# The first rows of an encoder layer: who prepares them, who issues their loads, and in which order and banks they are multiplied

## The chip, the cores and the metric

The kernel runs on one core of a Trainium2 chip, as one launch. The metric is the device time of that launch in microseconds. Five engines work side by side and meet at semaphores: TensorE (PE in the profile, with its weight loads as PEld), VectorE (DVE), ScalarE (ACT), GpSimd (POOL) and SyncE (SP), which issues most DMA transfers. ACT and POOL can issue transfers too.

## The reference

One layer of a hybrid encoder over 512 tokens of width 1024, float32 in and out: a half-step SwiGLU feed-forward, a mixer (dilated window attention in three groups, grouped-query attention with axial rotary, both gated and merged), a second half-step SwiGLU, and a final normalisation.

```python
def rmsnorm(x, g):
    y = x * lax.rsqrt(jnp.mean(x * x, axis=-1, keepdims=True) + EPS)
    return y * g

def swiglu(x, w1, w3, w2):
    return (jax.nn.silu(x @ w1) * (x @ w3)) @ w2

x = x + 0.5 * swiglu(rmsnorm(x, ffn1_norm), ffn1_w1, ffn1_w3, ffn1_w2)
h = rmsnorm(x, mix_norm)
x = x + hybrid_mixer(h, ...)
x = x + 0.5 * swiglu(rmsnorm(x, ffn2_norm), ffn2_w1, ffn2_w3, ffn2_w2)
return rmsnorm(x, final_norm)
```

D_FF is 2816. Only the beginning of the first feed-forward is touched by the change.

## The kernel before

Activations are held transposed, as eight tiles x0 to x7 of 128 features by 512 tokens. Every matrix product is made of three products of a shorter float format (float32r): an operand is split into a high part H (a rounded copy) and a low part L (the rest), and a product is H·H + L·H + H·L. On PE the weights' part is the stationary operand and the activations' part, 512 columns, the moving one. In the rows below hH and hL are the parts of the activations scaled by the norm's gain, wh and wl those of the weights, and wr is the raw weight tile as it was loaded. ACT usually makes the high part, DVE the low part. The factor 1/rms of the norm is applied after the product (tile R).

`layer` (L1264 on) opens the kernel. It allocates two raw and two split weight tiles, issues a few warm-up products on a zeroed tile (`idle`, L269) and then goes through the eight feature tiles d. For each it issues the load of x, for d below 4 also the load of that row's weights (in two pieces of 256 columns for d = 0, in one of 512 for the others), scales x into hH on ACT and hL on DVE (`norm_h`, L410 and L411), and splits the weights (L1274 on ACT, L1275 on DVE). "Row d" below is the d-th eighth of the sum over the 1024 features, with 12 products.

The first four blocks of 128 output features are computed together by `quad`: four PSUM banks, and for each row d and each of the four blocks three products (`mm3`, L262 to L264). After 28 of the 32 steps of `quad` the statistics product (`stat_r`, L441) stands on PE; it reads the sum of squares that ACT and DVE make after the last hH. Two PSUM pools of four banks exist: `psm` for blocks (tile name mm) and `psa` (tag aux) for the warm-up, the statistics and others. `quad` takes all of `psm`. The fifth block (`feat` with aux set, in `plain`) takes a bank of `psa`, the sixth takes the next of `psm`, that is the first bank of `quad`, which is empty when DVE has multiplied it by R (`done1`, L509). R is ready only after the statistics, so the results of `quad` are held until then.

PE runs in the order of the program text. The instructions of the other engines are put in order by a scheduler when the program is built. SP issues one DMA after the other; eight semaphores are used in turn by all transfers of SP and ACT, and an issue waits until the transfer that used its semaphore before has landed.

The kernel goes on with the rest of the first feed-forward (with a Strassen-like scheme of seven products for eight), the mixer and the second feed-forward; none of these lines is changed.

Of the kernel before, what the change touches and what calls it, by code (L numbers as in the profile page):

```python
# [13 lines left out]
AF = mybir.ActivationFunctionType  # L14
ALU = mybir.AluOpType
# [16 lines left out]
GAP_B = 1  # L32
LAG = 1
LAST = 2
WARM = 4
T = 512
D = 1024
NK = 8
# [11 lines left out]
G_FFN1, G_MIX, G_FFN2, G_FIN, G_BG = 0, 8, 16, 24, 32  # L50
# [16 lines left out]
def f32(t):  # L67
    return t.bitcast(F32)


class Layer:
    def __init__(self, ctx, tc, a):
# [9 lines left out]
        nc = self.nc  # L82
        c = self.cst
# [7 lines left out]
        self.mhalf, self.eps = small[:, 0:4], small[:, 4:5]  # L91
        nc.vector.memset(self.mhalf, -0.5)
        nc.vector.memset(self.eps, EPS)
        nc.scalar.activation(self.ones, self.ones, AF.Copy)
        self.r = c.tile([128, 8], F32, name="r")
        self.R = c.tile([128, T], F32, name="R")
        nc.gpsimd.memset(self.R, 0.0)
# [189 lines left out]
    def quad(self, name, done):  # L287
        banks = [self.bank() for _ in range(4)]
        for k in range(NK):
            if k % 2 == 0:  # L290
                H, L = self.weights(name, k // 2)
            for c in range(4):
                s = slice(512 * (k % 2) + 128 * c, 512 * (k % 2) + 128 * c + 128)
                self.mm3(banks[c], H[:, s], L[:, s], self.hH[k], self.hL[k], k == 0, k == NK - 1)
                if k == NK - 1:
                    done[c](banks[c])
                yield

    def token(self, name, n, toks, done):
        banks = [self.bank() for _ in toks]  # L300
# [102 lines left out]
            for _ in range(n):  # L403
                next(fill, None)

    def norm_h(self, d, g, n=T):
        nc = self.nc
        gc = self.par[:, g + d:g + d + 1]
        H, L, x = self.hH[d][:, :n], self.hL[d][:, :n], self.x[d][:, :n]
        self.lead = nc.scalar.activation(H, x, AF.Copy, scale=gc)  # L410
        nc.vector.scalar_tensor_tensor(L, x, gc, f32(H), op0=ALU.mult, op1=ALU.subtract)  # L411

    def norm_sq(self, d, pool=NK - 2):
        nc = self.nc
# [67 lines left out]
    def ffn_run(self, s, gin, gnext, hooks, out=None, side={}):  # L482
        nc = self.nc
        g, t, c, half = [], {}, {}, []
# [79 lines left out]
        def later(fn):  # L564
            return lambda ps: fn(ps) if held is None else held.append((fn, ps))
# [3 lines left out]
        def plain():  # L569
            if s == "a":  # L570
                yield from self.quad("w13a", [later(fn) for fn in (done1, done3) * 2])
            for f in range(2, first):
                yield from self.feat("w13" + s, 2 * f, later(done1), f == 2)
                yield from self.feat("w13" + s, 2 * f + 1, later(done3))

        def add(x, ps, R):
            if R is None:
# [28 lines left out]
        lo, n = first, 0  # L606
        for gi, hi in enumerate(ends):
            last = hi == NF
# [16 lines left out]
            n, lo = n + NK * len(g), hi  # L625
# [25 lines left out]
        sqs, first = [], iter(())  # L651
        for hf in range(2):
# [19 lines left out]
            first = norm(hf)  # L672
# [584 lines left out]
    def layer(self, out):  # L1257
        nc, tc = self.nc, self.tc
        for n in range(2):
            self.raws[n] = self.ring("wr", self.todo.pop(0), 0, n)  # L1260
            self.tiles.append(self.ring("wh", n, 0, n))
        self.idle(WARM, 256)
        for d in range(NK):
            if d > 3 and d % 2 == 0:  # L1264
                self.load(self.todo.pop(0))
            nc.sync.dma_start(self.x[d], self.a["x"][d])
            w = 0 if d > 3 else 512 if d else 256
            parts = [slice(512 * (d % 2) + s, 512 * (d % 2) + s + w) for s in range(0, 512, w)] if w else []
            for s in parts:
                nc.sync.dma_start(self.raws[d // 2][:, s], self.a["w13a"][d // 2][:, s])  # L1270
            self.norm_h(d, G_FFN1)
            for s in parts:
                raw, (H, L) = self.raws[d // 2], self.tiles[d // 2]
                nc.scalar.copy(H[:, s], raw[:, s])  # L1274
                nc.vector.tensor_sub(L[:, s], raw[:, s], f32(H)[:, s])  # L1275
        nc.sync.dma_start(self.ident, self.a["ident"])

        def squares():
            with tc.issue_after(self.lead.ins):
                for d in range(NK):  # L1280
                    self.norm_sq(d, 0)

        with tc.tile_pool(name="bt", bufs=1, side="right") as bp:
            hooks = {16: squares, 27: self.stat_r, 33: self.stat_R, "T": (22, 2)}
            self.bias_open(bp)
            side = {(0, d): lambda g=d: self.bias_rows(g) for d in range(3)}
            for h in range(8):
                side[(0, 4 + h) if h < 4 else (1, h - 4)] = lambda h=h: self.bias_spread(h)
            with ExitStack() as ctx:
                self.ffn_open(ctx, "a")  # L1290
                self.ffn_run("a", G_FFN1, G_MIX, hooks, side=side)
                self.freed = None
                self.wx = None
        self.fctx = ExitStack()
        self.mixer()
        self.ffn_run("b", G_FFN2, G_FIN, {3: self.stat_r, 5: self.stat_R}, out)
        self.wx = None
        self.fctx.close()
        self.hctx.close()
# [100 lines left out]
```

## Time and profile before

| | us |
|---|---|
| median of 3 runs (lowest, highest) | 1244.58 (1244.53, 1245.4) |
| profiled execution, its own time | 1244.16 |
| its span in the profile | 1242.4 |
| PE busy | 1233.9 (99%) |
| DVE busy | 906.8 (73%) |
| ACT busy | 605.8 (49%) |
| DMA, mean over the span | 154 GB/s |

The span goes from the first to the last instruction in the trace; the execution's own time holds 1.76 us more. In the rows of the timeline stand the start in us, the duration, the engine, the line, the operation, and what it writes and reads; "xN" is a count of merged instructions, and brackets at the end tell how long the engine had been idle and what ended that. ACTq, SPq and POOLq rows are issues of DMA transfers.

### The profile page before, as it was taken

How to read it: one execution, taken by the hardware profiler on the slowest of the kernel's cores; microseconds unless marked ns; L12 is line 12 of the kernel's file. 1: busy time of each engine (PE TensorE's matmuls, PEld its weight loads, DVE VectorE, ACT ScalarE, POOL GpSimd, SP SyncE). 2: the span in 40 equal slices, each digit the busy share in tenths (PEclk: the TensorE clock that was granted, in tenths of full speed). 3: DMA queues.
4: the chain of work that ended last, by engine and by line, in shares of the span. 5: the costliest groups of instructions: out<-in, count | busy, mean ns of one | idle time of the engine just before them, and what ended most of it. 6: DMA issues, size and time to landing. Idle time of an engine off the chain costs nothing.

```text
span 1242.4 us, 20511 instructions
## 1 busy us (share of the span) xinstructions
PE 1233.9 (99%) x8228; PEld 1116.0 (90%) x8228; DVE 906.8 (73%) x1371; ACT 605.8 (49%) x897; POOL 126.5 (10%) x131
## 2 busy tenths in 40 slices
PE   9999999999999999999999999999999999999998
PEld 7897999899899999988888888888899989988997
DVE  6985688468787887567746888865988757875874
ACT  7652365245464444454424446664665425532554
POOL 1111101000222110200001200000211001100001
PEclk9999999999999999999999999999999999999999
DMA  8785777241388982662232231267768536744222
GB/s 292 220 217 166 194 195 194 92 119 52 136 222 251 231 229 97 223 183 79 87 116 100 68 119 43 71 218 241 208 170 203 157 99 188 189 149 111 60 85 68
DMA packets 90224, 190.85 MB, mean 154 GB/s; under 512 B 12801, under 2 KB 18577, under 8 KB 90129
## 3 DMA queue, kind: packets, MB, share of 16 engines
q1 hardware_dynamic: 70912, 145.46, 34.5%
q0 software_dynamic: 18496, 43.54, 17.6%
q8 instruction: 64, 1.05, 0.4%
q10 hardware_dynamic: 720, 0.55, 0.1%
q14 instruction: 32, 0.25, 0.1%
HBM read 175.79 MB, written 17.38 MB: 155 GB/s over the span
## 4 chain that ended last, share of the span: by engine, by line
PE 92%; DVE 3%; DMA 2%; issue 1%; ACT 0%; SPq 0%; POOL 0%; POOLq 0%; ACTq 0%; DVEq 0%
PE mm L262 23%; PE mm L264 22%; PE mm L263 22%; PE Y L263 4%; PE Y L262 4%; PE Y L264 4%; PE X L263 2%; PE X L264 2%; PE X L262 2%; DMA wt<-in_w13b 1%; PE S L925 1%; PE mm L1001 1%; PE Tb L1137 1%; PE T L1012 1%; DVE wl L248 1%
## 5 line engine op out<-in xcount | busy, mean ns | idle before, releaser
L247 ACT CAST wh<-wr 128x1024 fp32r<-128x1024 f32 x133 | 139.6, 1050 | 182.2 <-PE mm L263 124.1
L248 DVE TENSOR_TENSOR wl<-wr,wh 128x1024 fp32r<-128x1024 f32 x133 | 163.0, 1225 | 52.1 <-ACT wh L247 51.5
L262 PE MATMUL mm<-hH,wh 128*128 128x256 f32 (+1 forms) x560 | 179.7, 321 | 0.4 <-DVE t L509 0.3
L264 PE MATMUL mm<-hH,wl 128*128 128x256 f32 (+1 forms) x560 | 177.0, 316 | 0.0
L263 PE MATMUL mm<-hL,wh 128*128 128x256 f32 (+1 forms) x560 | 176.9, 316 | 0.0
L262 PE MATMUL mm<-gg,wh 128*128 128x512 f32 (+1 forms) x440 | 166.4, 378 | 0.0
L263 PE MATMUL mm<-gg,wh 128*128 128x512 f32 (+1 forms) x440 | 165.9, 377 | 0.0
L264 PE MATMUL mm<-gg,wl 128*128 128x512 f32 (+1 forms) x440 | 165.9, 377 | 0.0
L262 PEld LDWEIGHTS mm<-hH,wh 128*128 128x128 f32 x560 | 105.2, 188 | 9.9 <-ACT wh L1274 1.1
L264 PEld LDWEIGHTS mm<-hH,wl 128*128 128x128 f32 x560 | 105.2, 188 | 8.4 <-DVE wl L1275 0.4
L263 PEld LDWEIGHTS mm<-hL,wh 128*128 128x128 f32 x560 | 105.3, 188 | 7.4 <-DVE hL L411 0.2
L247 ACT CAST wh<-wa 128x1024 fp32r<-128x1024 f32 x54 | 56.8, 1051 | 96.3 <-PE mm L263 46.1
L262 PEld LDWEIGHTS mm<-gg,wh 128*128 128x128 f32 x440 | 82.6, 188 | 16.6 <-PE mm L264 0.9
L264 PEld LDWEIGHTS mm<-gg,wl 128*128 128x128 f32 x440 | 82.6, 188 | 15.3
L263 PEld LDWEIGHTS mm<-gg,wh 128*128 128x128 f32 x440 | 82.6, 188 | 15.0
L247 ACT CAST wh<-ws 128x1024 fp32r<-128x1024 f32 x54 | 56.8, 1052 | 71.3 <-PE mm L263 49.3
L247 ACT CAST wh<-wt 128x1024 fp32r<-128x1024 f32 x54 | 56.8, 1052 | 64.9 <-PE mm L263 41.4
L262 PE MATMUL mm<-TH,wh 128*128 128x256 f32 x320 | 88.4, 276 | 0.0
L263 PE MATMUL mm<-TL,wh 128*128 128x256 f32 x320 | 88.3, 276 | 0.0
L264 PE MATMUL mm<-TH,wl 128*128 128x256 f32 x320 | 88.3, 276 | 0.0
L248 DVE TENSOR_TENSOR wl<-wt,wh 128x1024 fp32r<-128x1024 f32 x54 | 65.9, 1222 | 28.7 <-ACT wh L247 27.9
L581 DVE TENSOR_TENSOR u<-mm,R 128x512 f32<-128x512 f32 x40 | 27.7, 691 | 75.7 <-PE mm L264 75.5
(280 smaller groups left out, 3240.6 us busy)
## 6 DMA issues: line engine op xcount, KB each, us to landing
wr<-in_w2a SPq DMA_DIRECT2D x22, 512.0 KB, 3.3
wt<-in_w13b SPq DMA_DIRECT2D x22, 512.0 KB, 3.5
wa<-in_w13b SPq DMA_DIRECT2D x22, 512.0 KB, 3.3
wt<-in_w13b POOLq DMA_DIRECT2D x22, 512.0 KB, 6.0
wr<-in_w2b SPq DMA_DIRECT2D x22, 512.0 KB, 3.7
wt<-in_w13a SPq DMA_DIRECT2D x18, 512.0 KB, 3.8
wt<-in_w13a POOLq DMA_DIRECT2D x18, 512.0 KB, 7.1
wa<-in_w13a SPq DMA_DIRECT2D x18, 512.0 KB, 3.9
```

What stands on the lines that cost most here:

```text
L247: self.nc.scalar.copy(H, raw)
L248: self.nc.vector.tensor_sub(L, raw, f32(H))
L262: mm(out, lH, rH, start=start, stop=False, skip_group_check=more)
L263: mm(out, lH, rL, start=False, stop=False, skip_group_check=more)
L264: mm(out, lL, rH, start=False, stop=stop, skip_group_check=more)
L581: nc.vector.tensor_mul(u, ps, R)
L925: nc.tensor.matmul(*args, start=True, stop=True)
L1001: nc.tensor.matmul(oc, v, p, start=st, stop=sp)
L1012: nc.tensor.transpose(ps[:, 128 * b:128 * b + 128], P[h][:, c0 + 128 * b:c0 + 128 * b + 128], self.ident)
L1137: nc.tensor.transpose(pt[:, 128 * j:128 * j + 128], P[h, j][:, 128 * k:128 * k + 128], self.ident)
```

## The change

It has five parts, all at the beginning of the program. The order rows below come from the two built programs; they hold no times.

- ACT, not SP, issues the two pieces of the first row's weights, behind the load of the gains (par). ACT's first instruction (a copy of `ones`, which brings a table load) stands behind these issues now.
- For d = 0 hH is made in two halves: columns 0 to 255 on ACT, 256 to 511 on DVE. DVE also makes the high part of the first piece of the weights. hL of row 0 is made after that (`low`), and all wl of the first rows behind the last hL.
- `quad` orders the products of a row by kind for all rows but the last: four with hH·wh, four with hL·wh, four with hH·wl. The last row is as before. The steps at which other work is woven in stay 32.
- The warm-up has three products, not four.
- The sixth block takes a bank of `psa` as the fifth does.

On PE, at the first row: hH0 and hL0 are the parts of x0, wh_118 and wl_119 (wh_117 and wl_118 after) the first weight tile's parts, mm_195 to mm_198 the four banks. Before:

```order
L269 MATMUL warm_123<-R_92 128x256 x4
L262 MATMUL mm_195<-hH0_98,wh_118 128x512
L263 MATMUL mm_195<-hL0_106,wh_118 128x512
L264 MATMUL mm_195<-hH0_98,wl_119 128x512
L262 MATMUL mm_196<-hH0_98,wh_118 128x512
L263 MATMUL mm_196<-hL0_106,wh_118 128x512
L264 MATMUL mm_196<-hH0_98,wl_119 128x512
L262 MATMUL mm_197<-hH0_98,wh_118 128x512
```

And after the change, with what each row waits for (the waits of the first row's products stand here as the other engines' semaphores):

```order
L301 MATMUL mm_195<-hH0_97,wh_117 128x512 [waits DVE_49,Activation_49]
L301 MATMUL mm_196<-hH0_97,wh_117 128x512
L301 MATMUL mm_197<-hH0_97,wh_117 128x512 [waits Activation_49]
L301 MATMUL mm_198<-hH0_97,wh_117 128x512
L301 MATMUL mm_195<-hL0_105,wh_117 128x512 [waits DVE_49]
L301 MATMUL mm_195<-hH0_97,wl_118 128x512 [waits DVE_49]
L301 MATMUL mm_196<-hH0_97,wl_118 128x512
L301 MATMUL mm_197<-hH0_97,wl_118 128x512 [waits DVE_49]
```

The low parts moved from the second and third place of the row to the fifth and the ninth. The first product waits for both engines, the third for ACT's cast of the second piece of the weights.

On DVE, at the start, after the change (x_74 is x0, x_75 is x1):

```order
L418 TENSOR_SCALAR hH_97<-x_74,par 128x256
L1291 CAST wh<-wr 128x256
L425 SCALAR_TENSOR_TENSOR hL_105<-x_74,par,hH_97 128x512
L1295 TENSOR_TENSOR wl<-wr,wh 128x256 x2
L425 SCALAR_TENSOR_TENSOR hL_106<-x_75,par,hH_98 128x512
L1295 TENSOR_TENSOR wl<-wr,wh 128x512
```

The first two rows are new on DVE; the rest stood there before in this order. ACT has lost half of its first scaling and the first of its two casts of 256 columns.

On SP, at the start, before (in_x is the input, in_w13a the first feed-forward's weights; DMAHW0 to DMAHW7 are the eight semaphores):

```order
L1266 DMA x_74<-in_x 128x512
L1270 DMA wr<-in_w13a 128x256 x2
L1266 DMA x_75<-in_x 128x512
L1270 DMA wr<-in_w13a 128x512
L1266 DMA x_76<-in_x 128x512
L1270 DMA wr<-in_w13a 128x512
L1266 DMA x_77<-in_x 128x512 [waits DMAHW0_49]
L1270 DMA wr<-in_w13a 128x512 [waits DMAHW1_49]
```

After the change the row with x2 stands on ACT, between its load of par and its table load, and the rows behind it follow x_74 at once. The waits stay as they are: DMAHW0 belongs to the load of par, DMAHW1 to that of x_74.

The diff, cut to its core:

```diff
-WARM = 4
+WARM = 3
...
-        nc.scalar.activation(self.ones, self.ones, AF.Copy)
...
     def quad(self, name, done):
         banks = [self.bank() for _ in range(4)]
         for k in range(NK):
             if k % 2 == 0:
                 H, L = self.weights(name, k // 2)
...
-                self.mm3(banks[c], H[:, s], L[:, s], self.hH[k], self.hL[k], k == 0, k == NK - 1)
...
+            terms = [(w, h, c) for w, h in ((H, self.hH[k]), (H, self.hL[k]), (L, self.hH[k])) for c in range(4)]
+            for n, (w, h, c) in enumerate(terms):
+                self.nc.tensor.matmul(banks[c], w[:, s[c]], h, start=k == 0 and n < 4, stop=False)
+                if n % 3 == 2:
+                    yield
...
-    def norm_h(self, d, g, n=T):
+    def norm_h(self, d, g, n=T, first=False):
...
+        if first:
+            nc.scalar.activation(H[:, :256], x[:, :256], AF.Copy, scale=gc)
+            nc.vector.tensor_scalar(H[:, 256:], x[:, 256:], gc, None, op0=ALU.mult)
+            return
...
-                yield from self.feat("w13" + s, 2 * f + 1, later(done3))
+                yield from self.feat("w13" + s, 2 * f + 1, later(done3), f == 2)
...
+        for s in (slice(0, 256), slice(256, 512)):
+            nc.scalar.dma_start(self.raws[0][:, s], self.a["w13a"][0][:, s])
+        nc.scalar.activation(self.ones, self.ones, AF.Copy)
         self.idle(WARM, 256)
...
-            for s in parts:
+            for s in parts[:len(parts) * d]:
                 nc.sync.dma_start(self.raws[d // 2][:, s], self.a["w13a"][d // 2][:, s])
-            self.norm_h(d, G_FFN1)
+            self.norm_h(d, G_FFN1, first=d == 0)
             for s in parts:
                 raw, (H, L) = self.raws[d // 2], self.tiles[d // 2]
-                nc.scalar.copy(H[:, s], raw[:, s])
-                nc.vector.tensor_sub(L[:, s], raw[:, s], f32(H)[:, s])
+                (nc.scalar.copy if d or s.start else nc.vector.tensor_copy)(H[:, s], raw[:, s])
+                if d == 0 and s.start == 0:
+                    self.low(d, G_FFN1, T)
+                with tc.issue_after(self.lowest.ins):
+                    nc.vector.tensor_sub(L[:, s], raw[:, s], f32(H)[:, s])
```

`idle`, `feat`, `mm3` and `done1` are unchanged.

More of the change, by code (lines that the diff above doesn't have):

```diff
@@ L291, in quad @@
                 H, L = self.weights(name, k // 2)
-            for c in range(4):
-                s = slice(512 * (k % 2) + 128 * c, 512 * (k % 2) + 128 * c + 128)
-                self.mm3(banks[c], H[:, s], L[:, s], self.hH[k], self.hL[k], k == 0, k == NK - 1)
-                if k == NK - 1:
-                    done[c](banks[c])
-                yield
+            last = k == NK - 1
+            s = [slice(512 * (k % 2) + 128 * c, 512 * (k % 2) + 128 * c + 128) for c in range(4)]
+            if last:
+                for c in range(4):
+                    self.mm3(banks[c], H[:, s[c]], L[:, s[c]], self.hH[k], self.hL[k], False, True)
+                    done[c](banks[c])
+                    yield
+                continue
+            terms = [(w, h, c) for w, h in ((H, self.hH[k]), (H, self.hL[k]), (L, self.hH[k])) for c in range(4)]
+            for n, (w, h, c) in enumerate(terms):
+                self.nc.tensor.matmul(banks[c], w[:, s[c]], h, start=k == 0 and n < 4, stop=False)
+                if n % 3 == 2:
+                    yield
     def token(self, name, n, toks, done):
@@ L404, in weave, with low @@
                 next(fill, None)
-    def norm_h(self, d, g, n=T):
+    def norm_h(self, d, g, n=T, first=False):
         nc = self.nc
         gc = self.par[:, g + d:g + d + 1]
+        H, x = self.hH[d][:, :n], self.x[d][:, :n]
+        if first:
+            nc.scalar.activation(H[:, :256], x[:, :256], AF.Copy, scale=gc)
+            nc.vector.tensor_scalar(H[:, 256:], x[:, 256:], gc, None, op0=ALU.mult)
+            return
+        self.lead = nc.scalar.activation(H, x, AF.Copy, scale=gc)
+        self.low(d, g, n)
+    def low(self, d, g, n):
         H, L, x = self.hH[d][:, :n], self.hL[d][:, :n], self.x[d][:, :n]
-        self.lead = nc.scalar.activation(H, x, AF.Copy, scale=gc)
-        nc.vector.scalar_tensor_tensor(L, x, gc, f32(H), op0=ALU.mult, op1=ALU.subtract)
+        self.lowest = self.nc.vector.scalar_tensor_tensor(L, x, self.par[:, g + d:g + d + 1], f32(H), op0=ALU.mult, op1=ALU.subtract)
     def norm_sq(self, d, pool=NK - 2):
```

## Prediction

> **What bounds the kernel now.** I read the page first, then busy time by stretches, the chain of waits at the start, and the timeline of the first 36 us. The page names the engine:
>
> ```profile
> span 1242.4 us, 20511 instructions
> PE 1233.9 (99%) x8228; PEld 1116.0 (90%) x8228; DVE 906.8 (73%) x1371; ACT 605.8 (49%) x897; POOL 126.5 (10%) x131
> ```
>
> PE is busy for all but 8.5 us of the span, so an edit can only win there, where PE stands or waits for operands. The change touches the first 46 us, and these are the stretches in which it lies:
>
> ```profile
> 0.00:5.00 5.00, 3.68 (x9) 2.56 (x9) 0.47 (x4) 2.50 (x4) 0.73 (x5) 1.00 0.56 136
> 5.00:10.00 5.00, 4.91 (x18) 3.36 (x18) 3.28 (x7) 3.19 (x6) 0.00 (x0) 1.00 1.00 341
> 30.00:40.00 10.00, 9.73 (x45) 7.71 (x45) 9.12 (x11) 8.31 (x11) 3.66 (x3) 1.00 1.07 336
> ```
>
> The second column is PE's busy time; the last three are granted clock, DMA share and GB/s. PE is short in just these three stretches. But its ends are modelled, so waits are better taken from starts. The chain of waits through the start gives what ends last:
>
> ```profile
> 2.59 5.28 DMA wr<-in_w13a
> 7.89 0.63 ACT wh L1274
> 8.57 0.50 PE mm L262
> ```
>
> The weights of row 1 (the second eighth of the sum over k) are issued by SP at 2.59, land 5.28 us later, are cast by ACT, and let PE start row 1 at 8.57. What row 0 does before that is not on the chain. So an earlier first product is worth nothing unless row 1's weights come earlier too.
>
> Rows 0 and 1 on PE, from the timeline (start, duration, engine, line):
>
> ```profile
> 4.96 0.80 PE L262 MATMUL mm<-hH,wh 128*128 128x512 f32 x1
> 5.56 0.61 PE L263 MATMUL mm<-hL,wh 128*128 128x512 f32 x1
> 6.01 0.40 PE L264 MATMUL mm<-hH,wl 128*128 128x512 f32 x1
> 8.08 0.39 PE L264 MATMUL mm<-hH,wl 128*128 128x512 f32 x1
> 9.29 0.50 PE L264 MATMUL mm<-hH,wl 128*128 128x512 f32 x1
> 11.69 0.39 PE L262 MATMUL mm<-hH,wh 128*128 128x512 f32 x1
> 25.29 0.95 PE L441 MATMUL stat<-ones,acc 128*128 128x1 f32 x8
> ```
>
> Row 2 begins at 11.69 and the statistics at 25.29 stand 60 products later: 13.60 / 60 = 0.227 us a product, with no wait between. A row of 12 is 2.72. Row 1 took 11.69 - 8.57 = 3.12, so 0.40 of it is waiting, most of it before 9.29, where the third product needs the low part wl.
>
> **The change part by part.** *Row 0.* Its preparation before:
>
> ```profile
> 1.32 3.78 PE L269 MATMUL warm<-R 128*128 128x256 f32 x8 [1.32 <-POOL R L97]
> 3.90 0.72 ACT L410 ACTIVATE hH<-x,par 128x512 fp32r<-128x512 f32 x1 [1.22 <-DMA par<-in_par]
> 4.52 0.39 ACT L1274 CAST wh<-wr 128x256 fp32r<-128x256 f32 x1
> 4.65 0.75 DVE L411 SCALAR_TENSOR_TENSOR hL<-x,par,hH 128x512 fp32r<-128x512 f32 x1 [3.72 <-ACT hH L410]
> 5.28 0.40 ACT L1274 CAST wh<-wr 128x256 fp32r<-128x256 f32 x1 [0.36 <-DMA wr<-in_w13a]
> 5.32 0.82 DVE L1275 TENSOR_TENSOR wl<-wr,wh 128x256 fp32r<-128x256 f32 x2
> L990 DVE TENSOR_SCALAR P<-P,F 128x256 f32<-128x256 f32 x56 | 16.4, 347 | 0.0
> L410 ACT ACTIVATE hH<-x,par 128x256 fp32r<-128x256 f32 x4 | 2.0, 510 | 8.5 <-DVE x L1249 8.3
> ```
>
> Now ACT scales half of hH (0.51, the last row's mean) from 3.90 to 4.41, while DVE scales the other half (0.35, the row above it) to 4.25 and then casts the first quarter of the weights. No row shows a DVE cast of this shape; between half of the 0.35 and the 0.41 of a two-operand DVE instruction (0.82 for two) I take 0.35, the one-operand row. So PE can start at about 4.65 instead of 4.96 (4.5 to 4.75). The second half of the weights, cast by ACT at 5.28 before, holds the third product until 5.7 if it lands no earlier. hL follows on DVE from 4.6, about as now, and is needed only by the fifth product.
>
> PE's speed matters here. The weight loads show it:
>
> ```profile
> 4.96 0.29 PEld L262 LDWEIGHTS mm<-hH,wh 128*128 128x128 f32 x1 [0.58 <-ACT wh L1274]
> 6.01 0.19 PEld L262 LDWEIGHTS mm<-hH,wh 128*128 128x128 f32 x1
> ```
>
> A load takes 0.29 at 4.96 and 0.19 from 6.01 on, and products go from 0.45 apart (5.56 to 6.01) to 0.227. PE therefore gets fast at about 5.8, which is 4.5 us after the warm-up began at 1.32, although the granted clock reads 1.00 throughout. I assume that the opening stays at 5.8, as the warm-up still starts with the same fill of R. Then row 0 does (5.8 - 4.7) / 0.45 = 2.4 products slowly and 9.6 x 0.227 = 2.18 fast, and ends at 8.0; if the third product waits until 5.7, ten products from there end at 7.97. Both give 8.0, against 8.08 + 0.23 = 8.31 now.
>
> *Row 1's data.* SP's issues:
>
> ```profile
> 0.74 0.41 ACTq L86 DMA_DIRECT2D par<-in_par  x1
> 1.18 1.28 ACT L94 ACT_TABLE_LOAD   x1 [1.18 <-PEq L1391]
> 1.18 0.89 SPq L1270 DMA_DIRECT2D wr<-in_w13a  x2
> 2.12 0.43 SPq L1266 DMA_DIRECT2D x<-in_x  x1
> 2.59 0.43 SPq L1270 DMA_DIRECT2D wr<-in_w13a  x1
> 4.01 0.43 SPq L1266 DMA_DIRECT2D x<-in_x  x1
> 3.75:4.75 1.00, 1.00 (x4) 0.54 (x2) 0.10 (x1) 0.85 (x2) 0.00 (x0) 1.00 0.58 128
> 4.75:5.75 1.00, 1.00 (x3) 0.58 (x2) 1.00 (x3) 0.56 (x2) 0.00 (x0) 1.00 0.95 278
> ```
>
> The two issues of the first weights leave SP, so x and the weights of row 1 are issued at 1.18 and 1.65 instead of 2.12 and 2.59: 0.94 earlier. The fourth row of x (4.01) gains nothing, since it waits for the semaphore that par uses, and so do the issues behind it; they are needed only from row 3, which starts after 13. On ACT the two issues take 0.89 after par's, the table load follows to about 3.35 and the copy of ones to 3.55, ahead of 3.90; so the move costs ACT nothing, and a delay of more than 0.35 there would be paid in full. How much of the 0.94 reaches the landing, the trace does not show. The DMA engines stood at a share of 0.58 from 3.75 to 4.75, then at 0.95: 0.42 + 0.05 = 0.47 us of idle engine time can be filled. The bounds are 0 and 0.94; I take 0.6, between the hole and the issue time, nearer to the hole. The Trainium skill, DMA: Bandwidth & Descriptors, section "Issuing engines are not separate DMA queues", says that a second issuing engine saves sequencer time alone, since all transfers share the same 16 engines; by it the 0.94 is the most there is, and the share of 0.95 that follows agrees, while the 0.58 before it says that some issue time was really missing.
>
> Row 1's weights then land at 7.27 and PE can start row 1 at 8.57 - 0.6 = 7.97, just as row 0 ends. *Order by kind* takes the wait for wl out of row 1: wl is now asked for by the ninth product, 1.8 us after the first, while DVE finished it at 0.7 after PE's start of the row:
>
> ```profile
> 8.55 0.69 DVE L1275 TENSOR_TENSOR wl<-wr,wh 128x512 fp32r<-128x512 f32 x1 [0.44 <-ACT wh L1274]
> 21.43 3.07 DVE L421 TENSOR_TENSOR acc<-acc,sq 128x512 f32<-128x512 f32 x4
> ```
>
> Row 2 begins at 8.0 + 0.1 (the first product after a wait, as below) + 2.72 = 10.8, against 11.69: **0.9 us**. With the data no earlier it is 8.57 + 0.1 + 2.72 = 11.4, 0.3 us; with the whole 0.94 row 0 is the limit and it is 1.0. Next in line is the statistics product: the sum of squares ends at 24.50 on DVE (second row above), and PE would ask for it at 25.29 - 0.9 = 24.4. That chain starts from later transfers which move up with the filled hole, so I count 0 here, and at most 0.1.
>
> *The sixth block.* Its first product waits for a bank that DVE empties:
>
> ```profile
> 34.51 1.28 DVE L509 TENSOR_TENSOR t<-mm,R 128x512 f32<-128x512 f32 x2
> 34.59 0.39 PE L264 MATMUL mm<-hH,wl 128*128 128x512 f32 x1
> 35.25 0.50 PE L262 MATMUL mm<-hH,wh 128*128 128x512 f32 x1 [0.27 <-DVE t L509]
> 35.59 0.39 PE L263 MATMUL mm<-hL,wh 128*128 128x512 f32 x1
> ```
>
> From 34.59 to 35.59 stand two products that would take 0.45: 0.66 - 0.23 = 0.43 of wait and 0.34 - 0.23 = 0.11 of restart, **0.54 us**. In the other set the block takes the bank of the warm-up, which nobody reads. The wait moves to the seventh block, 24 products (5.4 us) later, while the bank is free at 35.2: hidden. Its weights were cast long before. Taking a wait away here gains 0 to 0.54; I take all. DVE and ACT swap a few instructions between 27 and 42 us; the results are wanted after 45, so nothing is counted for them. One warm-up product fewer costs nothing by itself.
>
> **The rivals.** *The engines are full anyway.* If row 1's data lands when it does now, the sum is 0.3 + 0.54 = 0.84. For it speaks the share of 0.95 and more from 4.75 on; against it the 0.58 before. The section of the Trainium skill named above would have it so wherever the engines, not the sequencer, are the limit.
>
> *PE stays slow longer: slower than before.* Three warm-up products of 3.78 / 4 = 0.94 end at about 4.2, PE stands for 0.4, and may stand again until 5.7. If PE's fast state needs an unbroken stretch, the 4.5 us start anew at 4.65 (or at 5.7), and it opens at 9.1 (10.2). Then row 0 does 9.8 products slowly and ends at 9.6 (10.25), row 2 begins at 12.3 (13.0) against 11.69, and with the 0.54 of the sixth block the kernel is 0.1 (0.75) slower. It decides from an opening later than 8.9. Against it: the gap is a tenth of the stretch. The Trainium skill, TensorE: Matmul & The Clock Gate, Part 1, describes half speed until a free-running window of about 3.4 us was busy; by it the next chance after 5.8 would be 9.2, an estimate from that page, close to the 9.1. No row here shows how busy a stretch has to be.
>
> *The bank edit only moves the wait*, to an operand or to the seventh block: 0.9 alone.
>
> **How the numbers follow.** Forecast: 0.9 + 0.54 = 1.44 us less, nothing later being tied to the clock on the wall, because SP and POOL wait for buffers that PE frees. The profiled execution took 1244.16 in all (span 1242.4 and 1.76 around it), so a profiled one would take 1242.7; the median of the runs, 1244.58, lies 0.42 above it, so I name **1243.1**, chance 0.52. Engines full: 1243.7, chance 0.22. Bank wait moved: 1243.7, chance 0.08. PE slow longer: 1244.7 to 1245.3, chance 0.13. Something else 0.05. Runs of before spread over 0.9 (1244.53 to 1245.4), so the range goes 0.7 below the forecast and up to the nearer end of the slow case: 1242.4 to 1244.8. A difference of 0.2% is 2.5 us, about what a measurement of this kernel tells from no change; no case but mishap reaches it: faster 0.03, same 0.93, slower 0.04.
>
> **What would show it.** First product at 4.6 to 4.75; first issue of row 1's weights on SP at 1.65 and landing near 7.3; loads of 0.19 from about 5.8; row 2 at 10.8; no idle time of PE before the sixth block, which then begins some 1.3 earlier than 35.25. Loads of 0.29 after 6.5, or row 1 starting at 8.5 again, would prove me wrong.

## The result, and the profile after

| | before | after |
|---|---|---|
| median (lowest to highest, runs) | 1244.74 (1243.19 to 1246.74, 22) | 1246.74 (1243.57 to 1249.37, 22) |
| profiled execution, its own time | 1244.16 | 1245.17 |
| its span | 1242.4 | 1243.4 |

The ratio is 1.0017, with a 95% interval of 1.0011 to 1.0023: the changed kernel is about 2.0 us slower. The forecast was 1.4 faster, and the range ended at 1244.8. Its runs also spread wider, over 5.8 us in place of 3.6. One thing has to be kept in mind with every row of its profile: at 1245.17 this execution is the third fastest of the 22, and by the runs below the larger part of what usually goes wrong did not go wrong in it.

The page and the stretches after, with the columns as shown of before:

```profile
span 1243.4 us, 20508 instructions
...
0.00:5.00 5.00, 2.93 (x6) 1.85 (x6) 0.47 (x4) 1.99 (x3) 0.73 (x5) 1.00 0.60 170
5.00:10.00 5.00, 3.60 (x15) 2.70 (x16) 4.01 (x8) 3.36 (x7) 0.00 (x0) 1.00 1.03 361
30.00:40.00 10.00, 10.00 (x48) 8.29 (x47) 8.79 (x11) 9.03 (x13) 3.66 (x3) 1.00 1.07 340
```

PE has lost 0.75 us of busy time before 5 us and 1.31 between 5 and 10; between 30 and 40 it is now full. The DMA engines move more in the first 10 us (170 and 361 GB/s against 136 and 341), so the hole that the prediction saw was filled, and PE got nothing from it. The chain of waits through the start says why:

```profile
1.67 4.95 DMA wr<-in_w13a
6.62 0.02 issue
6.64 0.41 ACT wh L1291
7.06 0.04 issue
7.10 7.10 PE mm L301 x30
```

Before, the chain went through row 1's weights. Now it goes through the second piece of row 0's, which ACT issues at 1.67 and which needs 4.95 us to land. The timeline of the first 36 us:

```profile
1.19 0.93 ACTq L1277 DMA_DIRECT2D wr<-in_w13a  x2
1.32 2.93 PE L268 MATMUL warm<-R 128*128 128x256 f32 x6 [1.32 <-POOL R L96]
1.65 0.42 SPq L1287 DMA_DIRECT2D wr<-in_w13a  x1
5.78 0.29 DVE L1291 CAST wh<-wr 128x256 fp32r<-128x256 f32 x1 [1.62 <-DMA wr<-in_w13a]
6.64 0.41 ACT L1291 CAST wh<-wr 128x256 fp32r<-128x256 f32 x1 [2.33 <-DMA wr<-in_w13a]
6.19 0.30 PEld L301 LDWEIGHTS mm<-hH,wh 128*128 128x128 f32 x2 [2.67 <-issue]
6.22 0.70 PE L301 MATMUL mm<-hH,wh 128*128 128x512 f32 x2 [1.98 <-DVE wh L1291]
9.51 1.07 PE L301 MATMUL mm<-hH,wh 128*128 128x512 f32 x4
12.23 1.07 PE L301 MATMUL mm<-hH,wh 128*128 128x512 f32 x4
35.35 0.39 PE L261 MATMUL mm<-hH,wh 128*128 128x512 f32 x1
```

DVE and ACT wait 1.62 and 2.33 us for the two pieces, which before were cast at 4.52 and 5.28. The first product stands at 6.22 in place of 4.96, rows 1 and 2 begin at 9.51 and 12.23 in place of 8.57 and 11.69: 0.54 late. The sixth block no longer waits for its bank (35.35, without a bracket, against 35.25), so at 36 us the two kernels are level, in this execution. The last 1.0 us of its difference comes half a millisecond later, in the mixer, where the partial softmax sums of two ways of cutting the sequence are exchanged through DRAM and DVE waits for them. The same DVE instruction before, and after:

```profile
556.78 0.17 DVE L970 TENSOR_TENSOR MN<-SO 128x16 f32<-128x16 f32 x1 [2.62 <-DMA SO<-d]
```

```profile
557.89 0.17 DVE L984 TENSOR_TENSOR MN<-SO 128x16 f32<-128x16 f32 x1 [3.65 <-DMA SO<-d]
```

So this profile left three candidates. **Q**: loads issued by ACT share the DMA engines with those that SP now issues alongside, and the first row's weights land late. **C**: PE needs a busy stretch before it gets fast, and three warm-up products that end at 4.25, followed by 2 us of standing, often do not give it one. **M**: the change makes the mixer's round trip late.

### The profile page after: what moved, and what is told of

It reads as the page before. It is cut to its first block, busy times and chain, and to the rows that moved or that the text cites. A ratio compares the mean times of both kernels' runs of the same rounds, so it can differ in the third digit from the quotient of the medians.

```text
span 1243.4 us, 20508 instructions
## 1 busy us (share of the span) xinstructions
PE 1233.3 (99%) x8226; PEld 1116.6 (90%) x8226; DVE 907.4 (73%) x1373; ACT 604.5 (49%) x896; POOL 125.8 (10%) x131
## 4 chain that ended last, share of the span: by engine, by line
PE 97%; issue 1%; DMA 1%; DVE 1%; ACT 0%; POOL 0%; ACTq 0%; POOLq 0%; SPq 0%; DVEq 0%
PE mm L261 24%; PE mm L263 23%; PE mm L262 23%; PE Y L263 4%; PE Y L262 4%; PE Y L261 4%; PE X L262 2%; PE X L263 2%; PE X L261 2%; PE mm L301 2%; PE S L939 1%; PE mm L1015 1%; PE Tb L1151 1%; PE T L1026 1%; PE Sb L263 1%
## 5 line engine op out<-in xcount | busy, mean ns | idle before, releaser
L261 PE MATMUL mm<-hH,wh 128*128 128x256 f32 (+1 forms) x532 | 168.3, 316 | 0.0
L261 PE MATMUL mm<-gg,wh 128*128 128x512 f32 (+1 forms) x440 | 166.6, 379 | 0.0
L263 PE MATMUL mm<-hH,wl 128*128 128x256 f32 (+1 forms) x532 | 166.1, 312 | 0.0
L262 PE MATMUL mm<-gg,wh 128*128 128x512 f32 (+1 forms) x440 | 166.1, 377 | 0.0
L262 PE MATMUL mm<-hL,wh 128*128 128x256 f32 (+1 forms) x532 | 165.9, 312 | 0.0
L261 PEld LDWEIGHTS mm<-hH,wh 128*128 128x128 f32 x532 | 99.9, 188 | 7.2 <-issue 0.9
L263 PEld LDWEIGHTS mm<-hH,wl 128*128 128x128 f32 x532 | 99.9, 188 | 6.8
L262 PEld LDWEIGHTS mm<-hL,wh 128*128 128x128 f32 x532 | 100.0, 188 | 6.1
L261 PEld LDWEIGHTS mm<-gg,wh 128*128 128x128 f32 x440 | 82.6, 188 | 16.5 <-PE mm L263 0.9
L262 PEld LDWEIGHTS mm<-gg,wh 128*128 128x128 f32 x440 | 82.7, 188 | 15.0
L261 PE MATMUL mm<-TH,wh 128*128 128x256 f32 x320 | 88.5, 277 | 0.0
L262 PE MATMUL mm<-TL,wh 128*128 128x256 f32 x320 | 88.5, 276 | 0.0
L247 DVE TENSOR_TENSOR wl<-wa,wh 128x1024 fp32r<-128x1024 f32 x54 | 65.9, 1220 | 23.4 <-ACT wh L246 23.3
```

The costliest lines, as they stand in the source:

```text
L247: self.nc.vector.tensor_sub(L, raw, f32(H))
L261: mm(out, lH, rH, start=start, stop=False, skip_group_check=more)
L262: mm(out, lH, rL, start=False, stop=False, skip_group_check=more)
L263: mm(out, lL, rH, start=False, stop=stop, skip_group_check=more)
```

## Experiments

All runs, with the median, lowest, highest and number of runs, and the ratio to the kernel before measured alongside. "Y" is the start of the first product of Y (L261 or L262, some 54 us) in the one profiled execution: a marker behind everything that the change touches.

| run | median us | ratio to before [95%] | Y |
|---|---|---|---|
| before | | | 54.53 |
| after | 1246.74 (1243.57 to 1249.37, 22) | 1.0017 [1.0011, 1.0023] | 54.49 |
| e1, after again | 1248.59 (1247.64 to 1251.5, 7) | 1.0030 [1.0018, 1.0042] | 57.10 |
| e2, after, loads on SP | 1244.93 (1243.23 to 1247.11, 11) | 1.0004 [0.9995, 1.0013] | 53.36 |
| e3, before, loads on ACT | 1245.85 (1243.85 to 1246.8, 11) | 1.0001 [0.9992, 1.0010] | 53.82 |
| e4, before, bank | 1244.08 (1242.18 to 1245.92, 11) | 0.9992 [0.9983, 1.0001] | 53.71 |
| e5, after, 5 warm-ups | 1245.95 (1244.6 to 1247.82, 11) | 1.0012 [1.0003, 1.0021] | 54.43 |
| e6, before, 3 warm-ups | 1246.08 (1244.41 to 1248.27, 11) | 1.0008 [0.9999, 1.0018] | 55.94 |
| e7, e2 with 4 warm-ups | 1244.6 (1243.33 to 1246.39, 11) | 1.0001 [0.9992, 1.0009] | 53.78 |
| e8, before, order by kind | 1244.93 (1243.47 to 1245.82, 11) | 0.9999 [0.9991, 1.0008] | 54.94 |
| e9, before, kind and bank | 1244.8 (1242.96 to 1246.44, 11) | 0.9991 [0.9982, 1.0000] | 53.93 |
| f1, before, no trip | 1243.19 (1242.9 to 1243.91, 11) | 0.9981 [0.9972, 0.9990] | 54.09 |
| f2, after, no trip | 1245.99 (1243.82 to 1247.06, 11) | 1.0000 [0.9991, 1.0009] | 57.73 |
| f3, e5, no trip | 1243.89 (1243.56 to 1246.38, 11) | 0.9987 [0.9979, 0.9996] | 54.62 |
| g1, f1 again | 1243.19 (1242.89 to 1243.68, 11) | 0.9981 [0.9972, 0.9990] | 54.80 |
| g2, e3, no trip | 1243.54 (1242.5 to 1245.35, 11) | 0.9981 [0.9972, 0.9990] | 54.17 |
| g3, e6, no trip | 1244.13 (1243.14 to 1244.45, 11) | 0.9989 [0.9980, 0.9998] | 55.61 |
| g4, e7, no trip | 1242.61 (1242.02 to 1242.9, 8) | 0.9976 [0.9966, 0.9986] | 54.00 |
| h2, g4, row 1's weights on ACT | 1243.12 (1242.46 to 1245.6, 11) | 0.9984 [0.9975, 0.9993] | 54.09 |

Run h1 stands apart and is told at the end. The kernel before, measured alongside, had medians of 1245.14 (e1 to e4), 1244.96 (e5 to e8), 1245.71 (e9 and f) and 1245.61 (g) over 29 to 33 runs, spread over 4.4 to 5.1 us, and 1245.16 (h) over 15. The ratio need not be the quotient of the medians: e3's median lies 0.7 us above, and its ratio is 1.0001.

### The change again, and single parts

e1 is the changed kernel once more, for a second profile.

> The changed kernel itself, once more, to see how much the start moves from one execution to the next. Theory Q (the first row's weights, issued on the second queue, share the DMA engines with the transfers that SP issues meanwhile and land late): the median is again about 2 us above before, the first product stands between 5.5 and 8 us, later than before's 4.96, and row 2 begins at or after 12.0 (11.69 before). Theory C (PE stays slow because it stands idle for 2 us): weight loads of 0.29 us are seen after 6.5 in this profile. Theory M (the loss is not at the start but in the mixer, where a wait for a DRAM round trip near 557 us took 1.1 us more in the changed kernel's profile): the start costs nothing and the 1.1 us is there again.

1248.59, 3.45 us above before. Its loads of weights on PE (start, duration; rows of four merged):

```profile
6.19 0.50 PEld L301 LDWEIGHTS mm<-hH,wh 128*128 128x128 f32 x2 [2.67 <-issue]
7.24 0.50 PEld L301 LDWEIGHTS mm<-hH,wh 128*128 128x128 f32 x2 [0.54 <-ACT wh L1291]
9.54 1.61 PEld L301 LDWEIGHTS mm<-hH,wl 128*128 128x128 f32 x4
11.25 1.46 PEld L301 LDWEIGHTS mm<-hH,wh 128*128 128x128 f32 x4
12.75 0.89 PEld L301 LDWEIGHTS mm<-hL,wh 128*128 128x128 f32 x4
```

The first product stands at 6.22 as in the profile of after, so the landing is the same. But there two loads took 0.30 at 6.19, here 0.50; four take 1.61 until 11.25 and 0.89 only from 12.75 on. Two executions of one program differ in when PE gets fast: by 6.2, or near 12.5. That costs 57.10 - 54.49 = 2.6 us at Y. C is at work, but not alone here: a further 2.2 us of this profile's difference arise behind Y.

e2 puts the first weights back on SP:

```diff
-        for s in (slice(0, 256), slice(256, 512)):
-            nc.scalar.dma_start(self.raws[0][:, s], self.a["w13a"][0][:, s])
...
-            for s in parts[:len(parts) * d]:
+            for s in parts:
```

> The changed kernel with the first row's weights issued by SP again, in their old place; halves, order by kind, three warm-up products and the bank stay. Theory Q: the loads land as before (4.1 and 5.25), the first product stands at 4.7, row 2 begins at 11.3 to 11.5 (0.2 to 0.4 earlier than before), the sixth block's 0.5 is gained too: 0.7 to 0.9 us faster than before, 2.5 to 3 faster than the changed kernel. Theory C: little change against the changed kernel, as the warm-up still ends at 4.2 and PE idles until 4.7; not faster than before. Theory M: 1 to 2 us slower than before, as the mixer is met at the same time.

The time is that of before, 3.7 us below e1 on the same chip: the queue is part of the cause, and C alone, by which little would change, is not the whole of it. The gain of 0.7 to 0.9 us against before that Q forecast did not come. In its profile the first product stands at 4.53 and Y 1.2 earlier than before, though the warm-up has three products.

e3 is the kernel before with these loads on ACT, and nothing else (the reverse of that diff, with the copy of `ones` behind the issues).

> The kernel before with one edit: ACT issues the first row's two loads, and its copy of ones stands behind them. Theory Q: the first product stands at 6 us or later, row 2 at 12.3 to 12.8, and the kernel is 0.8 to 2.5 us slower than before (the sixth block's 0.54 is still paid). Theory C: four warm-up products end at 5.1, so the idle time is about 1 us and less is lost: 0 to 0.5 us slower. Theory M: no difference at the start.

No change that can be told (1.0001, with 0.9992 to 1.0010). Its pieces were cast at 5.35 and 6.67, nearly as late as in after, but with four warm-up products PE was fast from its first product at 5.80. In this execution, the second fastest of the eleven (1244.0), the late landing alone does not make 2 us.

e4 is the kernel before with the sixth block's bank:

```diff
-                yield from self.feat("w13" + s, 2 * f + 1, later(done3))
+                yield from self.feat("w13" + s, 2 * f + 1, later(done3), f == 2)
```

> The kernel before with one edit: the sixth block takes a bank of the other set. All theories: PE does not wait before the sixth block, 0.54 us faster than before (0.3 to 0.6). If the wait only moves, no difference. Theory M: a shift of 0.5 us alone may make the mixer's wait come out otherwise, so the sign is open.

1.1 us below before by the medians; the interval ends at 1.0001. The wait for t is gone and no other has come in its place. PE's loads show that the opening is not fixed here either; it comes between these two rows, later than the 5.8 of before:

```profile
6.28 0.33 PEld L263 LDWEIGHTS mm<-hL,wh 128*128 128x128 f32 x1
6.69 0.19 PEld L264 LDWEIGHTS mm<-hH,wl 128*128 128x128 f32 x1
```

### The warm-up

e5 is the changed kernel with `WARM = 5`.

> The changed kernel with five warm-up products instead of three; nothing else. Theory Q (the first weights, issued on the second queue, share the DMA engines with everything that the first queue issues and land at about 5.7): the landing stays, the first product stays at 6.1 to 6.3, and the time stays that of the changed kernel, some 2 to 3.5 us above the kernel before. Theory C (PE loses its fast state because it stands idle from 4.25 to 6.2 after only three warm-up products): five products end at about 6.1 to 6.2 if they run slowly, or at about 5.7 if PE gets fast in them, loads are 0.19 from the first product on, row 2 starts at 12.1 to 12.4 every time, and the median is 1.5 to 3 us below that of the changed kernel: 0 to 0.7 us above the kernel before in the start, less 0.5 in the sixth block. Theory M (the loss sits in the mixer's DRAM round trip near 557 us, whatever the start does): second head pair's MN still at 558 or later, time 1 to 2.5 us above the kernel before.

1.0 us above before in place of 2.0 and 3.45. Q alone wanted no change against the changed kernel; C wanted a gain, and its row 2 begins at 12.16 as C said. Not as C said, its first two loads still take 0.50 at 5.83, and 0.30 for two is seen only from 7.06 on. That 1.0 is left was not expected.

e6 is the kernel before with `WARM = 3`, where the first product still comes at 5.00.

> The kernel before with three warm-up products instead of four; nothing else. Theory C: PE stands idle from about 4.25 to 4.96 and then works with small gaps; if any idle stretch of that size costs the opening of the fast state, loads stay at 0.29 or more behind 6.0 in the profile, row 2 starts at 12.3 or later (before 11.69), and the median is 0.5 to 2.5 us above the kernel before. If only the longer stand of the changed kernel (2 us) costs it, nothing changes: within 0.5 us of the kernel before, row 2 at 11.6 to 11.8. Theory Q says nothing here: no change.

1.1 us slower by the medians, with an interval that begins at 0.9999. The loads say more:

```profile
5.00 0.28 PEld L262 LDWEIGHTS mm<-hH,wh 128*128 128x128 f32 x1 [1.48 <-ACT wh L1274]
9.93 0.33 PEld L262 LDWEIGHTS mm<-hH,wh 128*128 128x128 f32 x1
10.36 0.20 PEld L263 LDWEIGHTS mm<-hL,wh 128*128 128x128 f32 x1
```

They stay at 0.33 until 9.93. With one warm-up product fewer, and a stand of 0.75 us (4.25 to 5.00), the opening comes between 9.93 and 10.36 in this profile, against 5.8 in that of before.

e7 is e2 with four warm-up products, e8 the kernel before with the order by kind alone.

> The changed kernel with the first weights issued on the first queue again (as in the kernel before) and four warm-up products: what stays of the change is the row shared by both engines, the order by kind and the sixth block's bank. Theories Q and C together: first product at 4.5 to 4.7, loads of 0.19 from at the latest 6.0, row 2 at 11.0 to 11.2, no wait before the sixth block: 0.5 to 1.2 us below the kernel before. Theory M: if the order by kind or the halves make the mixer's round trip late (MN of the second head pair at 558 or later), the gain of the start is given back there and the time is that of the kernel before or up to 1.5 us above it.

> The kernel before with the first products ordered by kind, nothing else. By the prediction's reading row 1 no longer waits for its low part: row 2 starts at 11.3 to 11.5 instead of 11.69, and the kernel is 0.2 to 0.4 us faster, which 5 rounds barely tell. Theory M as something systematic: MN of the second head pair at 558 or later (before 556.8), time 1 to 2 us above the kernel before. Theory M as chance: MN anywhere between 555.5 and 558, with no link to the start.

Neither can be told from before. Of e7, 0.5 to 1.2 us below before and loads of 0.19 from 6.0 were expected; in its profile loads are slow until about 7.2, and row 2 begins at 11.43 in place of 11.0 to 11.2. In the profile of e8 the term it was made for is there: row 1 takes from 9.21 to 12.10, 2.89 us where it took 3.12, and its low part is no longer waited for. Row 1 itself begins 0.64 later than in before, because its weights were cast later (8.54 against 7.89), so row 2 does not begin at 11.3 to 11.5, as was expected, but at 12.10:

```profile
9.21 1.21 PE L302 MATMUL mm<-hH,wh 128*128 128x512 f32 x4 [0.87 <-ACT wh L1281]
10.26 1.09 PE L302 MATMUL mm<-hL,wh 128*128 128x512 f32 x4
11.19 1.08 PE L302 MATMUL mm<-hH,wl 128*128 128x512 f32 x4
12.10 1.07 PE L302 MATMUL mm<-hH,wh 128*128 128x512 f32 x4
```

In these eight profiles the mixer's instruction of before's 556.78 stood anywhere from 555.71 (e4) to 562.00 (e1). M could be cause or noise.

### Without the mixer's round trip

To tell M apart the exchange through DRAM is left out: `merge_a` reads the sums of its own cut twice, and the DMAs of L951 to L963 go.

```diff
-        q.dma_start(nview(d0), SO[:, 0, 0:3, :])
...
-        nc.vector.tensor_tensor(MN, SO[:, 0, :, 0:2], SO[:, 1, :, 0:2], op=ALU.min)
+        nc.vector.tensor_tensor(MN, SO[:, 0, :, 0:2], SO[:, 0, :, 0:2], op=ALU.min)
```

> The kernel before without the mixer's round trip through DRAM: the partial maxima and sums of the first mixer's heads are not exchanged between the two ways of cutting the sequence, each head merges its own sums twice. This is the base for the next two, since it has no wait on that trip. All theories: 1 to 8 us below the kernel before, and its runs spread less, by 1.5 us in place of 4.

> The changed kernel with the same round trip left out as in the kernel named f1. Theory C (all of the loss is in the first 36 us, because PE's fast state opens late): 1.7 to 3 us above the base f1, as the changed kernel stands above the kernel before, and in the profile loads of the first rows stay slow past 9 us, or, where the opening came in time, the run lies within 0.3 us of the base. Theory M (the loss is in the mixer's round trip): within 0.5 us of the base.

> The changed kernel with five warm-up products, with the same round trip left out. Theory C: PE has no long stand before the first row, the fast state opens by about 8 us every time, and the median is within 0.4 us of the base f1: what is left of the landing at 5.7 and 6.6 (row 2 some 0.5 late) against the sixth block's 0.54. Theory Q alone, without the clock: 1.7 us or more above the base, as the changed kernel. Theory M: within 0.5 us of the base, as f2 then is too.

The spread of the base is 1.0 us, where the kernel before, measured alongside, spreads over 4.6. So most of the spread of the kernel before lies in that trip, and small terms can now be read. The changed kernel stands 1245.99 - 1243.19 = 2.80 us above the base. In the two profiled executions the difference is 1247.06 - 1242.90 = 4.2, of which 57.73 - 54.09 = 3.6 stand ahead of Y. **M falls** as the cause of the loss in the median: with no trip to be late, the loss is still there. With five warm-up products it is 0.70, so 2.1 of the 2.8 go with the warm-up. The loads of f2 in its profile, the slowest of its eleven runs, then those of f3:

```profile
5.53 0.50 PEld L301 LDWEIGHTS mm<-hH,wh 128*128 128x128 f32 x2 [2.01 <-issue]
7.49 0.50 PEld L301 LDWEIGHTS mm<-hH,wh 128*128 128x128 f32 x2 [1.46 <-ACT wh L1279]
11.51 1.61 PEld L301 LDWEIGHTS mm<-hH,wh 128*128 128x128 f32 x4
13.21 1.05 PEld L301 LDWEIGHTS mm<-hL,wh 128*128 128x128 f32 x4
```

```profile
5.55 0.30 PEld L301 LDWEIGHTS mm<-hH,wh 128*128 128x128 f32 x2 [0.34 <-issue]
7.23 0.30 PEld L301 LDWEIGHTS mm<-hH,wh 128*128 128x128 f32 x2 [1.38 <-ACT wh L1279]
```

f2 is slow through the whole of the first row and the first five products of the second, until past 13.2; f3 is fast from 5.55. Both stand again, 1.4 us, for the second piece of the weights. In f3 that does not take PE's full speed away once it is there (0.30 for two at 7.23). In f2 it falls into a stretch that might else have opened it, which is argued, not shown. Two of f3's eleven runs stand at 1246.1 and 1246.4; no profile shows what happened in them.

e9 is the kernel before with the order by kind and the bank.

> The kernel before with two parts of the change, the order by kind and the sixth block's bank, and nothing else (four warm-up products, all loads on the first queue, the first row prepared as before). By the single runs: no wait before the sixth block (0.5 to 0.7 us), no wait for the low part in row 1 (0.3): 0.6 to 1.0 us below the kernel before, the best version so far. If the two parts win the same time, 0.5. If the order by kind makes the mixer late (theory M): no gain, 0 to 1 above.

0.9 below before, with an interval of 0.9982 to 1.0000: about as good as e4, and no other kernel with the trip gained more than these two.

### The parts, without the trip

g1 repeats the base on the chip of g2 to g4; each of these holds one group of parts of the change.

> The kernel before without the mixer's round trip, as f1, on the chip of the next three: the base for them. 1242.8 to 1243.6 us, spread about 1 us.

> The base with one part of the change: the first weights issued on the second queue (the copy of ones behind them), four warm-up products as before. Theory Q (the late landing costs by itself): first product at 5.6 to 5.9, row 2 later than in the base, 0.3 to 1 us above the base. Theory C alone (only the lost opening costs): four products end at 5.1, PE stands 0.5 to 0.8; where the fast state has opened in time nothing is lost, where it has not, 2 to 3 us: a median within 0.3 of the base with some runs 2 us above it.

> The base with one part of the change: three warm-up products in place of four, the loads where they were. Theory C: the stretch from 1.3 to 4.25 is seldom enough, the next begins at 5.0, loads slow until 8.4 to 11.8 in most runs: 1 to 2 us above the base in the median, with few runs at the level of the base. The prediction's words (one warm-up product fewer costs nothing by itself): within 0.2 us of the base.

> The base with the rest of the change: the first row shared by both engines, the order by kind, the sixth block's bank; loads on the first queue, four warm-up products. The prediction's terms: 0.54 from the bank, 0.3 from the order by kind, 0 to 0.3 from the first product: 0.6 to 1.0 us below the base. If the sixth block's wait comes back elsewhere: 0.0 to 0.4 below.

The base came out at 1243.19 on both chips. Against it the queue alone stands 0.35 higher, three warm-up products alone 0.94, and the rest 0.58 lower. The 0.35 is not clear of the spread of g2's own runs (1242.5 to 1245.35, and by the ratio to before no difference from g1). Added up that is 0.7; together they cost 2.8. **The two interact**: in f2's profile the loads on ACT make PE stand, and after the shorter warm-up the stand falls ahead of the opening. That it is so in the other executions is concluded from the medians; one of each kernel was profiled. g3's words "costs nothing by itself" are the prediction's, and wrong by 0.94; ten of its eleven runs lie above the base's highest. Its last slow load and its first fast one:

```profile
9.39 0.33 PEld L264 LDWEIGHTS mm<-hH,wl 128*128 128x128 f32 x1
9.79 0.19 PEld L262 LDWEIGHTS mm<-hH,wh 128*128 128x128 f32 x1
```

### Why the loads land late

In the eleven profiles in which SP issues row 0's weights and ACT none, the first piece is cast between 4.04 and 4.56, never after a wait for it, and the second by 5.58 at the latest. In the seven in which ACT issues them, and SP's transfers follow at once, it is 5.10 to 5.78 and 6.60 to 7.04. In g4 the first piece, issued by SP, needs no wait on DVE; h2 is g4 with row 1's weights issued by ACT at 1.19, and row 0's still by SP.

```diff
+        nc.scalar.dma_start(self.raws[0][:, 512:], self.a["w13a"][0][:, 512:])
...
-            for s in parts:
+            for s in parts[:len(parts) * (d != 1)]:
```

> As g4 (the rest of the change, loads on the first queue, four warm-up products, no round trip; 1242.6), but row 1's weights are issued by ACT, at 1.2 in place of 2.6. Theory Q: row 1's weights land earlier by up to 1 us and take time from the first row's pieces, which land up to 0.7 later; first product 4.6 to 5.3, row 1 starts at 8.0 to 8.5 in place of 8.86; between 0.4 us below g4 and 0.4 above it. If the second queue is slower in itself: first row as in g4, row 1 no earlier, no change.

0.5 us slower than g4 by the medians, measured on another chip, and a little outside Q's forecast (0.4 at most). The cast of the first piece in g4, then in h2:

```profile
4.08 0.29 DVE L1277 CAST wh<-wr 128x256 fp32r<-128x256 f32 x1
```

```profile
5.07 0.29 DVE L1278 CAST wh<-wr 128x256 fp32r<-128x256 f32 x1 [0.92 <-DMA wr<-in_w13a]
```

The piece comes from the same queue, is issued at the same 1.19, and is cast 1.0 us later, after a wait for it, with row 1's weights in flight beside it; none of the eleven profiles above has it so late. Row 1's weights land 4.1 us behind their issue at 1.19, some 2.9 us earlier than in g4 (5.6 behind 2.59). That is Q: the queue that issues is not what is slow, and what is issued alongside takes engine time from what is needed first.

h1 was to show the same from the other side: g2, with two transfers of 32 bytes between the first and the second x on SP, so that SP's later loads keep their distance.

```diff
+        self.tiny = c.tile([1, 16], F32, name="tiny")
...
+            for n in range(2 * (d == 0)):
+                nc.sync.dma_start(self.tiny[:, 8 * n:8 * n + 8], self.a["par"][0:1, 0:8])
```

> As g2 (the base without the round trip, the first weights issued by ACT), but SP issues two transfers of 32 bytes between x of row 0 and x of row 1, so that x and weights of row 1 are issued at about 2.1 and 2.6, as in the kernel before, and not at 1.2 and 1.65. Theory Q (the engines are shared): ACT's two pieces land at 4.1 to 4.6 and 4.6 to 5.3, first product at 4.7 to 5.0, within 0.2 us of the base g1 (1243.2). If ACT's queue is slower in itself: casts stay at 5.1 or later for the first piece and 6.6 or later for the second, as in g2, and row 1 comes later too: 0.3 to 1 us above the base.

x of row 1 was issued at 1.83, not at the 2.1 hoped for, since a tiny issue takes 0.30. Half of the answer came. The first piece was there for its cast at 4.53, where g2 waited until 5.10 and no other profile with these loads on ACT has it before that, and the first product stood at 4.97, as Q forecast. The second came at 6.68 (7.04 in g2), which says nothing, since e3 with the same loads had it at 6.67:

```profile
4.53 0.39 ACT L1267 CAST wh<-wr 128x256 fp32r<-128x256 f32 x1
6.68 0.41 ACT L1267 CAST wh<-wr 128x256 fp32r<-128x256 f32 x1 [1.76 <-DMA wr<-in_w13a]
```

Its time says nothing of the queue: 1271.65 (1271.57 to 1272.19, 4 runs), slowed in a way that the last section tells.

## Why the prediction was wrong

**The first product at 4.65: wrong by 1.6 us, and it started the rest.** The step priced the halves, the DVE cast and ACT's issue time, and asked how much earlier row 1's data would land. It let row 0's second piece land "no earlier", but never asked whether both pieces land later, once x and weights of row 1 are in flight with them. They had been cast at 4.52 and 5.28 and came to 5.78 and 6.64. The trace of before held the hint: a DMA share of 0.58 between 3.75 and 4.75 was read as a hole to be filled at no cost, though row 0's second piece was still in flight there and ACT waited 0.36 us for it, until 5.28. The halves themselves did what was said: with the loads on SP the first product stands at 4.53 to 4.54 (e2, e7, g4), against 4.76 to 5.00 in the eight profiles with the loads on SP and no halves.

**"I assume that the opening stays at 5.8": the step that failed most.** It was one draw taken for a constant. In all profiles with four or five warm-up products loads were fast by 7.6 at the latest (e9), in g4 from about 4.6 on. In the six with three they were fast by 6.2 in after and e2, and only from between 9.4 and 14 in e1, e6, f2 and g3. The earliest opening (g4), then the latest with the longer warm-up (e9, two rows), where four loads take 1.61 before the opening and 0.88 behind it:

```profile
4.49 0.43 PEld L301 LDWEIGHTS mm<-hH,wh 128*128 128x128 f32 x2
```

```profile
6.37 1.36 PEld L302 LDWEIGHTS mm<-hL,wh 128*128 128x128 f32 x4
7.77 0.88 PEld L302 LDWEIGHTS mm<-hH,wl 128*128 128x128 f32 x4
```

Counted from the start of the busy stretch, the slow part took 3.2 to 3.4 us (g4) to 6.2 (e9) with the longer warm-up, 4.5 to 4.9 from 4.89 in g3, 4.9 to 5.4 from 5.00 in e6, and 5.7 to 6.8 from 7.49 in f2. The Trainium skill, TensorE: Matmul & The Clock Gate, Part 1, has a free-running window of 3.4 us that must have been busy. By an estimate from that section of the Trainium skill the opening falls one to two windows, 3.4 to 6.8 us, behind the start of a stretch; these rows agree, with g4 at the lower end or a little below it.

**"One warm-up product fewer costs nothing by itself": 0.94** (g3 against g1), and some 2.1 for two products fewer where the first row also comes late (f2 against f3).

**Row 1's data 0.6 earlier** moved nothing by itself: row 0 became the limit, and in g2, where only the queue is changed, the median is 0.35 worse, which its spread does not tell from no change. The term was mis-sized too: in after row 1's weights landed 4.8 us behind their issue at 1.65, at about 6.45 in place of 7.87. That is 1.4 us, more than the 0.94 that was taken for the most, and it goes with row 0's pieces coming later. PE got nothing of it.

**The bank, the order by kind and the halves: right, in sum a little too large.** Without the trip they win 0.58 together; the terms were 0.54, 0.3 and little for the halves, and the bank's wait did not come back. The rival that the bank only moves the wait falls.

**The rival "PE stays slow longer" was the true one, at a chance of 0.13, and too small.** It let the stretch start at 4.65 or 5.7 and open 4.5 us later, at 9.1 or 10.2, for 0.1 to 0.75 us net. Measured is a stretch from 6.2, or from 7.5 behind a second stand that the rival had end at 5.7, and an opening up to 6.8 later: 2.0 us with the trip, 2.8 without. Against it stood that the gap was "a tenth of the stretch". With a gap of 0.64 us (4.25 to 4.89 in its profile) ten of g3's eleven runs lie above the base.

What stays open: how busy a stretch has to be. In after and e2 PE had full speed by 6.2 with three warm-up products, in after behind nearly 2 us of standing. An estimate with the window of 3.4 us from the section of the Trainium skill named above: no such stretch in after can be busier than 2.93 / 3.4 = 86%, and it opened; in e6, which opened near 10.2, the window before its last one ran from 3.4 to 6.8 and was busy for 0.85 + 1.8 = 2.65 us, 78%, and did not. In g3, which opened near 9.7, it ran from 2.9 to 6.3 and was busy for 1.35 + 1.4 = 2.75 us, 81%, and did not either. No run was made to find the bound between. And with five warm-up products a loss remains: e5 stood 1.0 above before, and all of f3's runs lie above the base's median, 0.7 in theirs, though the queue alone (g2) and the rest (g4) would add up to -0.2. This was not split further.

## What to carry to other kernels

In this kernel a warm-up had to reach to the first real product with little or no stand between, and with a margin: whatever delays that product later, a load above all, can cost the opening as well. When a load that is needed first is moved to another queue, ask what will now be in flight beside it; the same bytes earlier are only a gain for what is on the chain. Where runs of one kernel spread over more than the effect, find the stage that spreads, leave it out on both sides, and measure the parts there: the third warm-up product's 1.1 us (e6) did not clear its interval with the trip, and its 0.94 (g3) put ten runs of eleven above the base's highest without it.

## What was not expected of the hardware

When PE gets its full speed differs between executions of one program: two profiles had it by 6.2 and near 12.5 us, while the granted clock read 1.00 in all these stretches (in e1 from 5 to 14 us too).

The second surprise is h1, 28 us above g2's median in all its runs, while the kernel before ran at its usual 1245.16 beside it. The loss is spread over the run. Two successive products of 256 columns in g2, then two of other tiles in h1:

```profile
59.97 0.28 PE L261 MATMUL X<-hH,wh 128*128 128x256 f32 x1
60.08 0.28 PE L262 MATMUL X<-hL,wh 128*128 128x256 f32 x1
```

```profile
59.98 0.28 PE L262 MATMUL mm<-TH,wh 128*128 128x256 f32 x1
60.10 0.28 PE L263 MATMUL mm<-TL,wh 128*128 128x256 f32 x1
```

0.11 us apart in g2, 0.12 in h1. Over all products of one width, from start to start, the medians are 0.113 and 0.120 for 256 columns, and 0.227 and 0.233 for 512. Summed up, the 4,688 products of 256 columns take 21.4 us more in h1's profile than in g2's and the 2,712 of 512 columns 7.9 us more, together about the 28.6 us by which the spans differ. Not all are slower: between 155 and 310 us those of 512 columns stand 0.227 apart in both. Besides the two transfers, the edit puts a tile of 64 bytes a partition ahead of all later tiles in SBUF. That their place, not the transfers, slows PE is possible, and not shown: no run here moved the tile alone.
